# A pooling trunk layer: an opening that normalizes its operands before the first product

## The chip, the core and the metric

The kernel runs on one core of a Trainium2 chip. The core has a matrix engine (TensorE, PE in the profile; PEld is its weight load), a vector engine (VectorE, DVE), a scalar engine (ScalarE, ACT), GpSimd (POOL) and a queue engine (SyncE, SP) that here only issues transfers; ACT and POOL issue transfers too. On-chip data lie in SBUF, matmul results in eight PSUM banks of 128 x 512 float32. The metric is the time of one execution in microseconds; lower is better.

## What is computed

One layer: RMS norm, a causal pooling mixer with a gate, the residual, and a last RMS norm. The input `x` is 4096 x 1024 float32; the second mixer of the source is not used at this depth.

```python
def rms_norm(x, w):
    y = x * rsqrt(mean(x * x, axis=-1) + 1e-6)
    return y * w

def pool_mixer(h, in_w, group_w, group_b, scale, out_w):
    u, gate = split(h @ in_w, 2, axis=-1)                    # in_w: 1024 x 2048
    pooled = trailing_mean(u by group, windows 2/4/8/16) - u # 4 groups of 256 channels
    mixed = einsum('bsgc,gcd->bsgd', pooled, group_w) + group_b
    y = mixed * scale * silu(gate)
    return y @ out_w                                         # 1024 x 1024

h = x + pool_mixer(rms_norm(x, norm_w), ...)
out = rms_norm(h, final_norm_w)
```

## The kernel before

**Products.** Every float32 operand is split into a rounded part and a residual (`split`: an ACT copy of 128 x 1024, then a DVE subtraction), and a product is made of three matmuls (`mm3`). The large products follow Winograd's form of Strassen's scheme: seven block products, P1 to P7, in the order P1, P2, P6, P7, P5, P4, P3 (`ORDER_IN`). Steps "a" make the gate columns' half of the input product for four blocks of 1024 tokens, steps "b" the other half, and steps "o" the output product in eight blocks of 512 tokens. `group_w` is folded into `in_w` ahead (`fold`: matmuls of 128 x 256, line 334), because pooling acts on tokens and the group map on channels.

**One step.** `load`, `form` (the Strassen sums on DVE), `split_step`, `run` (`product_in`: eight groups of six matmuls, each group one half `h` of the inner dimension and one PSUM bank `ct`; then `evict_in`). P1 goes bank by bank, and its results are copied to banks 4 to 7 by the eviction, which frees banks 0 to 3 for P2 to add to. Bank 7 also serves as scratch for the spread below.

**Normalization.** The operands come transposed, with tokens along the free dimension, so each needs the factor of its token as a row that is equal in all partitions. `load_row` and `square_row` read `x` a second time, by rows, and sum its squares on ACT; `stats` and `rsqrt` make the factor (a root on ACT, the rest on DVE). In the first block `spread_rs` turns the factors of one half (512 tokens) into a row: an ACT copy and a DVE difference split them, two DVE products put them on a diagonal (`ident`), two matmuls with a matrix of ones (line 396) spread them into bank 7, and ACT copies them to `rstd`. Later blocks store and reload the factors through DRAM (`store_rs`, `load_rstd`), a block ahead.

**The opening before the change.** While weights arrive, 14 matmuls on zeros warm up PE. Eight folds of 16 matmuls follow: four with `gw[0]` and four with `gw[1]`, on weights `ru[q, k]` of 512 KB each, which take four buffers in turn. The operands of P1 and P2 of the first block (the first half's tokens) are used raw, without their factor; `evict_in` multiplies the results by the factor on DVE instead, and `normalize_raw` normalizes the operands afterwards for the Strassen sums and stores them to `sd` for steps "b". All loads go out on SP in the order of the program: the first half's rows (`load_row(0, 0, j)`) behind the third and fourth folds, then the second half's rows, P2's operand (`load(1)`), its weights (`g1`), and the four operands of P6 (`load(2)`). The first spread is written ahead of P1's second group, the second one ahead of its sixth.

**Order.** The program is written in one stream; a scheduler puts the instructions of each engine into an order, by the place in the program and by when it expects them to be ready. `tc.high_priority()` moves a part ahead; `tc.issue_after(i)` keeps a part behind instruction `i` on the same engine. Engines work through their queues in that order.

**The end.** The last block's rows are finished in halves: `late_factor` makes a row's factor, `late_half` applies it (one half on ACT, one on DVE) and stores both.

Of the kernel before, what the change touches and what calls it, by code (L numbers as in the profile page):

```python
# [10 lines left out]
F32 = mybir.dt.float32  # L11
# [49 lines left out]
def kernel(  # L61
# [82 lines left out]
    def sub(dst, a, b):  # L144
        nc.vector.tensor_tensor(out=dst, in0=a, in1=b, op=ALU.subtract)  # L145
# [7 lines left out]
    def split(dst, src):  # L153

        copy(dst[:, 0], src)
        sub(dst[:, 1], src, dst[:, 0].bitcast(F32))
# [30 lines left out]
    def rsqrt(dst, tmp, ms):  # L187

        nc.scalar.activation(tmp, ms, AF.Sqrt)
        nc.vector.reciprocal(out=dst, in_=tmp)  # L190
        mul(tmp, dst, ms)
        mul(tmp, tmp, dst)
        nc.vector.tensor_scalar(
            out=tmp, in0=tmp, scalar1=-0.5, scalar2=1.5, op0=ALU.mult, op1=ALU.add
        )
        mul(dst, dst, tmp)
# [111 lines left out]


# [10 lines left out]
    def load_wut(q, k, by=2):  # L320
        r = take("p (k t c) -> p k t c", early5, k=2, t=4)
        for kk in range(0, 2, by):
            nc.sync.dma_start(
                out=r[:, kk : kk + by],
                in_=wut[q, k + kk : k + kk + by].rearrange("k p t c -> p k t c"),
            )
        return r

    def fold(q, k, g, r, ps2, o, on_vector=False):

        for kk in range(2):
            for j in range(2):
                for t in range(2):
                    nc.tensor.matmul(  # L334
# [5 lines left out]
                    )  # L340
            if on_vector:
                last = nc.vector.tensor_scalar(
                    out=o[:, kk], in0=ps2[kk], scalar1=norm_c[k + kk], scalar2=None, op0=ALU.mult
                )
            else:
                last = nc.scalar.activation(o[:, kk], ps2[kk], AF.Copy, scale=norm_c[k + kk])
        give(r)
        return last
# [21 lines left out]
    def stats(b, half):  # L370
        ms = small.tile([P, 4], F32, tag="ms", name=f"ms{b}_{half}")
        nc.vector.tensor_scalar(
            out=ms, in0=sums[b, half], scalar1=1.0 / D, scalar2=EPS, op0=ALU.mult, op1=ALU.add
        )
        tmp = small.tile([P, 4], F32, tag="tmp", name=f"tmp{b}_{half}")
        rs = small.tile([P, 4], F32, tag="rs", name=f"rs{b}_{half}")
        rsqrt(rs, tmp, ms)
# [4 lines left out]

    def spread_rs(half, rs):

        hl = small.tile([P, 2, 4], F32R, tag="hl", name=f"hl{half}")
        split(hl, rs)
# [8 lines left out]
        for s in range(2):  # L395
            nc.tensor.matmul(
                banks[7], ones, r[:, s, 0], start=s == 0, stop=s == 1, skip_group_check=True
            )
# [24 lines left out]
    def split_halves(us, saved=None, by_pool=False):  # L423
        ts = []
        for h, u in enumerate(us):
            t = next_op("p (s a b) -> p s a b", s=2, a=2)
            split(t, u)
            if saved is not None:
                (nc.gpsimd if by_pool else nc.scalar).dma_start(out=saved[h], in_=u)
# [30 lines left out]
    def form_in(q, b, i):  # L460

        s = xs[b]
        if i in (P1, P2):
            if q == 0 and b > 0:
                for u in s["11" if i == P1 else "12"]:
                    normalize(b, 0, u)
        elif i == P6:
            s["2"] = [take(pool=early if q == 0 and b == 0 else None) for _ in range(2)]
# [16 lines left out]
    def split_in(q, b, i):  # L485
        s = xs[b]
        key = {P1: "11", P2: "12", P6: "2", P7: "21", P5: "11", P4: "22", P3: "12"}[i]
        raw = b == 0 and i in (P1, P2)
        t = split_halves(s[key], None if q or raw else sd[b].get(i), b == 0)
# [6 lines left out]

    def normalize_raw(i):

        for h, u in enumerate(xs[0]["11" if i == P1 else "12"]):
            normalize(0, 0, u)  # L500
            nc.gpsimd.dma_start(out=sd[0][i][h], in_=u)
# [7 lines left out]
    def mm3(ps, lt, r, start, stop):  # L509

        for n, (a, b) in enumerate(((lt[0], r[0]), (lt[0], r[1]), (lt[1], r[0]))):
            nc.tensor.matmul(  # L512
                ps, a, b, start=start and n == 0, stop=stop and n == 2, skip_group_check=True
            )
# [3 lines left out]
    def product_in(i, t, sets, by_bank, between=None):  # L518
# [4 lines left out]
        for n, (h, ct) in enumerate(halves):  # L523
# [3 lines left out]
            for kk in range(2):  # L527
                mm3(
                    ps[ct],
                    (w[i][h][:, 0, kk, c], w[i][h][:, 1, kk, c]),  # L530
                    (t[h][:, 0, kk], t[h][:, 1, kk]),
                    i in (P1, P7) and h == 0 and kk == 0,
                    h == 1 and kk == 1,
                )
# [81 lines left out]
    def evict_in(b, q, i, sets):  # L616
        ps = sets[bank_of[i]]
        last = None
        if i in (P1, P2) and b == 0 and q == 0:
            if i == P2:  # L620
                ev["11"] = [take() for _ in range(2)]
            for c, u in enumerate(sets["y"] if i == P1 else cells(ev["11"])):
                mul(u, ps[c], rstd[0][:, 0])
            if i == P2:
                for u in ev["11"]:
                    last = copy(u, u, AF.Silu)
# [526 lines left out]
```

## Time and profile before

| | |
|---|---|
| median of 3 runs | 966.03 us (965.89 to 967.31) |
| the profiled execution | 964.39 us; its span, first to last instruction, 962.6 us |
| PE busy | 949.7 us, 4190 matmuls |
| DVE, ACT busy | 748.4 and 453.0 us |
| POOL | 6.7 us, 16 instructions: 4 memsets and 12 transfers issued |
| transfers | 177.0 MB; in the first 62 us 23.8 MB |
| granted PE clock | 0.997 of full speed, mean |

The profile is of one execution. "Busy" is the time in which an engine had an instruction under way; matmuls are pipelined, so PE counts as busy while they follow each other. A line of a timeline is start, duration, engine, line of the kernel, operation, what it writes and reads, and how often; in brackets stands how long the engine was idle before and what ended that. Lines of helpers (142, 145, 148, 151) are shared by many uses, which the tile names tell apart: `op` is a split operand, `w` a weight, `st`, `vt` and `early` are buffers.

### The profile page before, as it was taken

Reading aid. Unit: us, or ns where it says so; the run is one execution under the profiler, and the core shown is the slowest. Engines: PE = TensorE matmul, PEld = TensorE weight load, DVE = VectorE, ACT = ScalarE, POOL = GpSimd, SP = SyncE. Lnnn points to the kernel's source line nnn. Section 1 sums busy time; section 2 is a strip of 40 time slices with the busy share of each in tenths; the row PEclk is TensorE's granted clock in tenths of the full one; section 3 lists DMA queues with packets and bytes.
Section 4 is the critical chain, followed back from the end, with each engine's and each line's share of the span. In section 5 each row is a group of like instructions: output and inputs, shape, how many; then the busy total and the mean of one; then the engine's idle time right before and its main releaser. Section 6 shows DMA issues by size and latency. Waiting matters only on the chain.

```text
span 962.6 us, 11058 instructions
## 1 busy us (share of the span) xinstructions
PE 949.7 (99%) x4190; PEld 785.5 (82%) x4190; DVE 748.4 (78%) x919; ACT 453.0 (47%) x677; POOL 6.7 (1%) x16
## 2 busy tenths in 40 slices
PE   9999999999999999999999999999999999999996
PEld 8778888888888888888888888888888888888885
DVE  4699994893895997696697599499978667677675
ACT  5849447347445555345345445553423424324233
POOL 0110000000000000000000000000000000000000
PEclk9999999999999999999999999999999999999998
DMA  9965864564656646016614733645746436356022
GB/s 337 408 264 157 305 237 163 210 240 137 213 219 226 233 156 237 1 45 218 240 44 165 263 119 131 219 151 178 259 141 212 162 123 230 108 187 218 22 88 88
DMA packets 67685, 177.01 MB, mean 184 GB/s; under 512 B 6704, under 2 KB 24240, under 8 KB 67632
## 3 DMA queue, kind: packets, MB, share of 16 engines
q1 hardware_dynamic: 61728, 156.37, 46.8%
q10 hardware_dynamic: 4176, 13.65, 3.5%
q0 software_dynamic: 1728, 6.29, 1.6%
q8 instruction: 33, 0.54, 0.2%
q14 instruction: 20, 0.16, 0.1%
HBM read 116.50 MB, written 59.78 MB: 183 GB/s over the span
## 4 chain that ended last, share of the span: by engine, by line
PE 78%; DVE 13%; DMA 5%; ACT 3%; issue 1%; DVEq 0%; SPq 0%; ACTq 0%
PE bank L512 75%; PE bank L334 2%; DVE op L145 2%; DVE vt L142 2%; DMA st<-wvd 2%; DVE st L148 1%; DVE st L145 1%; DMA rd<-rs 1%; DVE st L598 1%; DVE w L145 1%; DMA st<-rd 1%; DVE st L261 1%; DVE vt L145 1%; DVE w L209 1%; DVE st L142 1%
## 5 line engine op out<-in xcount | busy, mean ns | idle before, releaser
L512 PE MATMUL bank<-op,w 128*128 128x512 f32 x2688 | 611.7, 389 | 2.5 <-ACT op L151 2.1
L512 PEld LDWEIGHTS bank<-op,w 128*128 128x128 f32 x2688 | 504.0, 188 | 109.1 <-ACT op L151 2.6
L512 PE MATMUL bank<-w,op 128*128 128x512 f32 (+1 forms) x1356 | 305.0, 387 | 0.0
L512 PEld LDWEIGHTS bank<-w,op 128*128 128x128 f32 x1356 | 253.0, 188 | 52.0
L151 ACT ACTIVATE op<-st 128x1024 fp32r<-128x1024 f32 x117 | 123.2, 1056 | 142.0 <-PE bank L512 112.2
L145 DVE TENSOR_TENSOR op<-st,op 128x1024 fp32r<-128x1024 f32 x117 | 141.5, 1217 | 38.7 <-ACT op L151 38.3
L151 ACT ACTIVATE op<-vt 128x1024 fp32r<-128x1024 f32 x49 | 51.8, 1059 | 92.2 <-PE bank L512 72.9
L142 DVE TENSOR_TENSOR vt<-vt 128x1024 f32<-128x1024 f32 (+6 forms) x72 | 87.7, 1227 | 0.1
L142 DVE TENSOR_TENSOR st<-bank,st 128x512 f32<-128x512 f32 x78 | 53.1, 686 | 36.9 <-PE bank L512 36.6
L145 DVE TENSOR_TENSOR op<-vt,op 128x1024 fp32r<-128x1024 f32 x49 | 59.8, 1220 | 21.7 <-ACT op L151 21.7
L151 ACT ACTIVATE vt<-bank 128x512 f32<-128x512 f32 x90 | 52.6, 595 | 46.1 <-PE bank L512 42.5
L142 DVE TENSOR_TENSOR vt<-bank,vt 128x512 f32<-128x512 f32 (+1 forms) x83 | 55.1, 677 | 15.0 <-PE bank L512 10.8
L145 DVE TENSOR_TENSOR st<-st,st 128x1024 f32<-128x1024 f32 x35 | 42.3, 1217 | 13.0 <-DMA st<-wvd 11.2
L151 ACT ACTIVATE bank<-bank 128x512 f32<-128x512 f32 x44 | 25.5, 582 | 33.9 <-PE bank L512 30.1
L145 DVE TENSOR_TENSOR w<-st,w 128x1024 fp32r<-128x1024 f32 x22 | 26.5, 1220 | 16.4 <-ACT w L151 16.2
L148 DVE TENSOR_TENSOR st<-st,st 128x1024 f32<-128x1024 f32 (+1 forms) x18 | 20.4, 1160 | 19.6 <-DMA st<-rd 18.3
L151 ACT ACTIVATE w<-st 128x1024 fp32r<-128x1024 f32 x22 | 23.1, 1059 | 22.9 <-PE bank L512 15.4
L151 ACT ACTIVATE st<-bank 128x512 f32<-128x512 f32 x36 | 21.2, 596 | 21.1 <-PE bank L512 19.1
L593 DVE SCALAR_TENSOR_TENSOR vt<-vt,vt 128x1024 f32<-128x1024 f32 x24 | 29.2, 1217 | 0.1
L334 PE MATMUL bank<-early,early 128*128 128x256 f32 x128 | 27.8, 379 | 0.0
L334 PEld LDWEIGHTS bank<-early,early 128*128 128x128 f32 x128 | 24.3, 190 | 3.3
L598 DVE SCALAR_TENSOR_TENSOR st<-vt,colt,st 128x512 f32<-128x512 f32 x36 | 25.6, 742 | 0.0
(116 smaller groups left out, 449.7 us busy)
## 6 DMA issues: line engine op xcount, KB each, us to landing
st<-in_x SPq DMA_DIRECT2D x34, 512.0 KB, 4.5
vt<-in_x SPq DMA_DIRECT2D x25, 512.0 KB, 4.5
st<-sd SPq DMA_DIRECT2D x25, 512.0 KB, 5.4
st<-in_xt SPq DMA_DIRECT2D x24, 512.0 KB, 6.1
sd<-st ACTq DMA_DIRECT2D x19, 512.0 KB, 6.4
st<-yd SPq DMA_DIRECT2D x19, 512.0 KB, 3.7
yd<-st SPq DMA_DIRECT2D x18, 512.0 KB, 2.9
out<-st SPq DMA_DIRECT2D x17, 512.0 KB, 4.8
```

What stands on the lines that cost most here:

```text
L142: nc.vector.tensor_tensor(out=dst, in0=a, in1=b, op=ALU.add)
L145: nc.vector.tensor_tensor(out=dst, in0=a, in1=b, op=ALU.subtract)
L148: nc.vector.tensor_tensor(out=dst, in0=a, in1=b, op=ALU.mult)
L151: return nc.scalar.activation(dst, src, func)
L209: nc.vector.scalar_tensor_tensor(out=dst[:, 1], in0=u, scalar=c, in1=dst[:, 0].bitcast(F32), op0=ALU.mult, op1=ALU.subtract,)
L261: nc.vector.scalar_tensor_tensor(out=u[:, j], in0=u[:, j], scalar=cs[j], in1=other[:, j], op0=ALU.mult, op1=op)
L334: nc.tensor.matmul(ps2[kk][:, j * 256 : (j + 1) * 256], r[:, kk, 2 * j + t, :], g[:, 2 * j + t, :], start=(t == 0), stop=(t == 1),)
L512: nc.tensor.matmul(ps, a, b, start=start and n == 0, stop=stop and n == 2, skip_group_check=True)
L593: nc.vector.scalar_tensor_tensor(out=s[:, :, at : at + H], in0=s[:, :, at : at + H], scalar=1.0 / win, in1=v[:, :, HIST:], op0=ALU.mult, o ...
L598: nc.vector.scalar_tensor_tensor(out=sg[:, j], in0=s[:, j, at : at + H], scalar=bias_c[2 * grp + j], in1=sg[:, j], op0=ALU.add, op1=ALU.mult,)
```

## The change

- **Operands of P1 and P2** are normalized before they are split, as in the other blocks; the DVE products in `evict_in` and `normalize_raw` are gone. `split_halves` stores the normalized operands to `sd` at once, on POOL's queue.
- **Loads.** The first half's four rows go out ahead of the last weights of the first four folds, the identity and `gw[1]`; `in_w`'s rows later. The first fold weights are issued half on ACT's queue and half on SP, ahead of `cols`. P2's operand and weights now go out ahead of the second half's rows.
- **Factors.** The first half's squares stand behind the first fold, the first spread behind the sixth fold's matmuls. The second spread is written behind P1 and held behind its last matmul; P2's second group is held behind it (`behind`).
- **Root.** A root on one column at the start brings its table in; `rsqrt` takes mean and epsilon into the root itself and does its multiplications on POOL, one reciprocal on DVE. `rsqrt` serves all blocks and the output's norm.
- **Folds.** Outputs are taken after the weights' buffer is given back; in the last four folds DVE evicts one of the two banks. 8 warm-up matmuls instead of 14.
- **Later weights.** P7's residuals, and the weights made in the first block's steps, are held on DVE behind the latest operand split.
- **End.** The second row half of P4 is finished behind the factor of P3's first row half, and DVE's part of `late_half` is held behind the latest addition or mean.

```diff
-    for c in range(14):
+    for c in range(8):
...
+    scrap = const.tile([P, 1], F32, name="scrap")
+    nc.scalar.activation(scrap, eps, AF.Sqrt)
+    def rsqrt(dst, tmp, ms, ss):
+        nc.scalar.activation(tmp, ss, AF.Sqrt, bias=eps, scale=1.0 / D)
+        nc.gpsimd.tensor_scalar(
+            out=ms, in0=ss, scalar1=1.0 / D, scalar2=EPS, op0=ALU.mult, op1=ALU.add
+        )
         nc.vector.reciprocal(out=dst, in_=tmp)
-        mul(tmp, dst, ms)
-        mul(tmp, tmp, dst)
-        nc.vector.tensor_scalar(
+        nc.gpsimd.tensor_tensor(out=tmp, in0=dst, in1=ms, op=ALU.mult)
+        nc.gpsimd.tensor_tensor(out=tmp, in0=tmp, in1=dst, op=ALU.mult)
+        nc.gpsimd.tensor_scalar(
             out=tmp, in0=tmp, scalar1=-0.5, scalar2=1.5, op0=ALU.mult, op1=ALU.add
         )
-        mul(dst, dst, tmp)
+        nc.gpsimd.tensor_tensor(out=dst, in0=dst, in1=tmp, op=ALU.mult)
...
     def spread_rs(half, rs):
-        split(hl, rs)
+        copy(hl[:, 0], rs)
+        nc.gpsimd.tensor_tensor(
+            out=hl[:, 1], in0=rs, in1=hl[:, 0].bitcast(F32), op=ALU.subtract
+        )
...
+        with tc.issue_after(latest[0]):
+            for s in range(2):
+                spread_done[0] = nc.tensor.matmul(
+                    banks[7], ones, r[:, s, 0], start=s == 0, stop=s == 1, skip_group_check=True
+                ).ins
...
-        raw = b == 0 and i in (P1, P2)
-        t = split_halves(s[key], None if q or raw else sd[b].get(i), b == 0)
+        t = split_halves(s[key], None if q else sd[b].get(i), b == 0)
...
+            with tc.issue_after(behind) if behind and n == 1 else nullcontext():
...
-        if i in (P1, P2) and b == 0 and q == 0:
-            if i == P2:
-                ev["11"] = [take() for _ in range(2)]
-            for c, u in enumerate(sets["y"] if i == P1 else cells(ev["11"])):
-                mul(u, ps[c], rstd[0][:, 0])
-            if i == P2:
-                for u in ev["11"]:
-                    last = copy(u, u, AF.Silu)
-        elif i == P1:
+        if i == P1:
...
+                if i == P3 and j == 0:
+                    late_half(*partial.pop("waiting"))
+        if final and i == P4:
+            partial["waiting"] = (half, 1, n, factors.pop())
...
-    ru[0, 0] = load_wut(0, 0, by=1)
-    for h, k in chunks[1:]:
-        ru[0, k] = load_wut(0, k)
-    g0.append(load_rows(in_w, 0, D))
-    gw[1] = load_group_w(1)
+    ru[0, 0] = load_wut(0, 0, (nc.scalar, nc.sync))
+    nc.scalar.dma_start(out=colt, in_=cols)
+    ru[0, 4] = load_wut(0, 4)
+    ru[0, 2] = load_wut(0, 2)
+    load_row(0, 0, 0)
+    load_row(0, 0, 1)
+    ru[0, 6] = load_wut(0, 6)
+    load_row(0, 0, 2)
+    load_row(0, 0, 3)
     ident = take(pool=early)
     nc.sync.dma_start(out=ident.rearrange("p a b -> p (a b)")[:, 0:P], in_=eye)
+    gw[1] = load_group_w(1)
     for n, (h, k) in enumerate(chunks):          # the first four folds
...
         ru[1, k] = load_wut(1, k)
         if n == 0:
             load(0)
+            for j in range(4):
+                square_row(0, 0, j)
+            with tc.high_priority():
+                rs = stats(0, 0)
+        elif n == 1:
+            for hh in range(2):
+                g0.append(load_rows(in_w, 2 * hh, D))
...
-    for j in range(4):
-        load_row(0, 1, j, early if j < 1 else None)
     load(1)
     g1 = [load_rows(in_w, 4 + 2 * h, D) for h in range(2)]
+    for j in range(4):
+        load_row(0, 1, j, early if j < 3 else None)
+    load(2)
...
     for n, (h, k) in enumerate(chunks):          # the last four folds
+        o = fold(1, k, gw[1], ru[1, k], banks[2 * (n % 2) : 2 * (n % 2) + 2], early5, (0,))
         nc.gpsimd.dma_start(out=wvd[k // 2], in_=o)
         give(o)
+        if n == 0:
+            for hh in range(2):
+                split_scaled(w[P1][hh], g0[hh], pair(norm_c, hh, 0))
+        elif n == 1:
+            with tc.high_priority():
+                spread_rs(0, rs)
+            form(0)
+            split_step(0)
+            second_side(0)
     give(gw[1])
+    second_side(1)
+    form(1)
     split_step(1)
     for h in range(2):
         split_scaled(w[P2][h], g1[h], pair(norm_c, h, 1))
+    for j in range(4):
+        square_row(0, 1, j)
+    with tc.high_priority():
+        rs = stats(0, 1)
+    def spread_second():
+        with tc.high_priority():
+            spread_rs(1, rs)
-    run(0, {1: lambda: spread(0), 5: lambda: spread(1)})
+    run(0, {8: spread_second})
...
     for h in range(2):
         for key in ("21", "22"):
-            normalize(0, 1, xs[0][key][h])
-    form(2)
-    split_step(2)
-    run(1)
-    normalize_raw(P2)
+            normalize(0, 1, s[key][h])
+        sub(s["21"][h], s["11"][h], s["21"][h])
+        sub(s["2"][h], s["22"][h], s["21"][h])
+        split_up[2] += split_halves([s["2"][h]])
     give(rstd.pop(0))
+    run(1, behind=spread_done[0])
     for h in range(2):
-        split(w[P7][h], v0[h])
-        give(v0[h])
+        copy(w[P7][h][:, 0], v0[h])
+    with tc.issue_after(latest_split[0]):
+        for h in range(2):
+            sub(w[P7][h][:, 1], v0[h], w[P7][h][:, 0].bitcast(F32))
+            give(v0[h])
...
         if kind == "a" and b == 0:
-            rest_of_first(n)
+            with tc.issue_after(latest_split[0]):
+                rest_of_first(n)
```

## The prediction

> **What bounds the kernel now.** I read the page first, then what TensorE waited for, then the opening in order of time.
>
> ```profile
> PE 949.7 (99%) x4190; PEld 785.5 (82%) x4190; DVE 748.4 (78%) x919; ACT 453.0 (47%) x677; POOL 6.7 (1%) x16
> ```
>
> PE is busy for 949.7 of 962.6 us and no product is removed, so the change can win only from the 12.9 us in which PE is idle. The waits of PE (engine, line, releaser: us in total, times, longest) place 5.2 us of them; 7.7 us lie behind the last matmul (954.9 to 962.6).
>
> ```profile
> PE bank L512 <- ACT op L151: 2.1, 1, 2.1
> PE bank L900 <- DVE op L898: 1.5, 1, 1.5
> PE bank L396 <- DVE w L389: 1.2, 1, 1.2
> PE bank L512 <- DVE op L145: 0.4, 2, 0.2
> ```
>
> The timeline of PE from 30 to 62 us (start, duration, instruction, idle before):
>
> ```profile
> 33.84 1.72 PE L512 MATMUL bank<-op,w 128*128 128x512 f32 x6
> 36.80 0.50 PE L396 MATMUL bank<-w,w 128*128 128x512 f32 x1 [1.24 <-DVE w L389]
> ...
> 37.74 10.86 PE L512 MATMUL bank<-op,w 128*128 128x512 f32 x47
> ...
> 49.25 9.49 PE L512 MATMUL bank<-op,w 128*128 128x512 f32 x41
> 60.88 1.42 PE L512 MATMUL bank<-op,w 128*128 128x512 f32 x5 [2.14 <-ACT op L151]
> ```
>
> PE stands 1.24 us for the first spread (L396) and 2.14 us before P6, which ends at 72.6. From there to 955 it waits 0.4 us at most, so what is won at P6's end is won for the program. Why P6 waited is in the windows (busy PE, PEld, DVE, ACT, POOL; clock; DMA share; GB/s) and the timeline of DVE:
>
> ```profile
> 50.00:54.00 4.00, 4.00 (x19) 3.32 (x18) 4.00 (x6) 1.36 (x2) 0.00 (x0) 1.00 1.04 410
> 58.00:62.00 4.00, 1.86 (x9) 1.14 (x7) 4.00 (x5) 3.46 (x5) 0.59 (x2) 1.00 0.99 405
> ```
> ```profile
> 51.37 1.22 DVE L148 TENSOR_TENSOR vt<-vt,st 128x1024 f32<-128x1024 f32 x1
> 52.50 3.49 DVE L148 TENSOR_TENSOR st<-st,st 128x1024 f32<-128x1024 f32 x3
> ```
>
> The second spread is done at 50.4; then DVE does four normalizations and four differences at 1.22 us one after the other, and P6's operand is the last. DMA is full as well (about 410 GB/s from 30 to 60 us), so 512 KB (0.524 MB) more ahead of a load make it land 1.28 us later. The DMA view, asked in windows around single issues, gives issue to landing (13.1 us for the last two rows of the second half, issued at 22.8 and 23.8; 16.1 for the last loads of P6's operand, issued up to 37.5):
>
> ```profile
> vt<-in_x SPq DMA_DIRECT2D x2, 512.0 KB, 13.1
> st<-in_xt SPq DMA_DIRECT2D x3, 512.0 KB, 16.1
> ```
>
> So the second half's rows have landed by 37.4 (13.65 for the last one alone) and the last operand by 53.6.
>
> **The change part by part.**
>
> *Start.* Warm-up loses 6 matmuls at 0.23 us, 1.4 us; one half of the first weights goes out on ACT's queue at 0.7 instead of SP's at 1.8, ahead of `cols`, which is needed only at the first eviction (8.3). The folds can begin near 5.3 instead of 6.4. But four row loads now stand ahead of fold weights: the seventh block landed 5.5 us after its issue at 16.96, at 22.5, and lands 4 x 1.28 = 5.1 us later, at 27.6, less about 0.5 for the earlier start, 27.1. In the trace that fold begins at 6.41 + 6 x 3.46 = 27.2 (16 matmuls at 0.216 each). It begins no earlier now, and the folds end near 27.1 + 6.9 = 34.0, where they ended at 34.2. The 1.1 us is lost again; nothing to 1.1 is the range.
>
> *First factors.* The first rows land by 15 (nine blocks of 512 KB at 1.28 us, from 3), four squares at 1.24 us are hidden under folds, the spread follows fold 6 at about 27. Then one ACT copy of 0.6, two normalizations of 1.22, two splits (ACT 1.05, DVE 1.22): ready near 33, beside folds. DVE has 9.8 us of work between 24.3 (first `in_w` rows) and 34. P1 starts on the folds and its stop of 1.24 us is gone, as are the 0.36 and 0.3 us in which PE turned between spread and product. With 48 matmuls at 0.227 us, 10.9 us, P1 ends near 44.9 (now 47.2, after 6, 1 and 41 of the 47 matmuls above). Cover gone, each us by which DVE is late costs one. The eight evictions of 0.69 us on DVE become ACT's (0.6 each) and shorten no wait by themselves. The table load (1.28 us, at 33.2) goes from ACT's chain to the start, where another stood.
>
> *Second factors.* This is what is late next. Their rows move behind four loads (two operands, two weight tiles), 4 x 1.28 = 5.1 us, and the stores of P1's and P2's inputs, until now put off, share the engines earlier; with the wvd stores up to four more have gone by then, again 5.1. The rows land between 42.5 (no store ahead) and 47.6 (all ahead); I take 47.0, as POOL's queue has the stores ready from 24 to 38. Then square 1.24, root 0.2, reciprocal 0.17, four small POOL operations, factor copy 0.21, two products of 0.65 and hand-overs of 0.1: with 0.2 us for a POOL operation 4.6 us, so the spread is at 51.6 and the factors are there at 52.7. PE does not idle all of 44.9 to 51.6: four of P2's eight groups (6 matmuls, 1.36 us each) depend on neither the spread nor bank 7's eviction, and today's order shows that late work is passed: the second spread is written ahead of P1's sixth group and runs behind P2's first. So P2 runs to 50.3, waits 1.3, spreads 0.5, and ends near 57.5 (now 58.7).
>
> *P6.* From 52.7: two normalizations, two differences (4 x 1.22) and the ACT copy of 1.05 give its first operand at 58.6, its residual 1.2 later; the second half follows 5 DVE steps later, at 64.7 plus 1.2, where PE's first 5.4 us are done at about 65.2. P6 ends near 71.4, against 72.6: 1.2 us won. DVE's slots are free for this: P2's evictions leave it.
>
> *POOL.* Five small operations of each of two factor chains here, six later ones and 14 output chains go from DVE (0.16 to 0.19 us each) to POOL, whose page shows no such operation. Its nearest rows are 0.10 us for a 128x1 memset and 0.53 for issuing a store. I take 0.2, as both are short and the data is 4 columns; the range runs from 0.1 to 1.2 for a start and a hand-over that these rows do not show, and for store issues ahead in its queue. In the later blocks nothing waits: the factors go through DRAM there (4.5 and 5.1 us) and PE never stood.
> By the Trainium skill's GPSIMD Engine Reference, section 4.1, elementwise work belongs on the Vector engine, since POOL is about twice as slow for two inputs. That gives an estimate of 0.33 us, and the second factors would come about 0.5 us later; no operation of this trace can confirm it.
>
> *Waits by order.* `behind` holds P2's second group until the spread: priced above. `latest_split` puts weight splits behind operand splits on DVE, where P7 is 11 us away: nothing. If that cover went, a split is 1.22.
>
> *End.* DVE's last chain stands behind a 0.75 us product: the square root ends at 956.8, the reciprocal starts at 957.25.
>
> ```profile
> 956.46 0.75 DVE L798 SCALAR_TENSOR_TENSOR st<-st,columns,st 128x512 f32<-128x512 f32 x1
> 956.50 0.29 ACT L780 ACTIVATE columns<-columns 128x1 f32<-128x1 f32 x1
> ...
> 957.25 0.15 DVE L782 RECIPROCAL columns<-columns 128x1 f32<-128x1 f32 x1
> ```
>
> The P4 half moves behind the next factor chain, which frees 0.7 us earlier: I take 0.3 (nothing to 0.45).
>
> **Sum.** 1.2 + 0.3 = 1.5 us. The profiled execution took 964.4 us (span 962.6, 1.8 around it) and becomes 962.9; it lies 1.6 us below the median of 966.0, which becomes 964.5.
>
> **Rivals.**
> 1. *All hidden.* Stores give way, the rows land at 42.5, the spread fits P1's end. P2 ends at 56.2, P6 waits only for its last loads (53.6 plus one store, 54.9) and ends near 68.7: 3.9 us, with the end 4.2, 961.8. For: `behind` fits such a time. Against: a full DMA.
> 2. *PE queued behind the spread.* If it is placed after P2's first group, PE waits from 46.3 to 51.6 and does seven groups after it: P2 ends at 61.6, P6 at 72.7; with the end 965.8 (966.6 for rows at 47.6).
> 3. *POOL is slow* (slower). Five steps of the second chain are on POOL. At p us each P6 ends 5(p - 0.2) later: the gain of 1.5 is gone at p = 0.5, and 0.2% slower is reached at 0.9. At 1.2 us it costs 5, so 969.5. For: no row shows such an operation, and POOL also issues eight stores in that stretch. Against: its memset of 0.1 us.
> 4. *Folds on a slow PE.* The first eight warm-up matmuls are 0.43 us apart, the rest 0.23; eight may just not be enough. Sixteen folds at half speed cost 3.5 us, of which the lead of 1.1 pays part, and all later stages move by up to 2.4: 965 to 967.
> The Trainium skill's TensorE: Matmul & The Clock Gate, Part 1, says that the warm-up takes about 3.4 us of time in a window that runs freely; eight at 0.43 are just that, and by this rule it may go either way.
>
> **Numbers.** Chances: forecast 0.37, all hidden 0.23, queued 0.14, slow POOL 0.20, slow folds 0.06. A measurement of this kernel can tell about 0.2%, 1.9 us, from no change. Faster by more is "all hidden" and a third of the forecast (below 964.1): 0.35. Slower by more is slow POOL and the upper ends of cases 2 and 4: 0.23. The rest, 0.42, is within. The likeliest case alone spans 963.5 to 966 (rows at 45 to 47.6). The range leaves out the lower half of case 1 and the upper half of case 3: 961.9 to 968.5.
>
> **What the profile would show.** Right: folds that wait for weights in their second half and end at 34; no PE wait at P1's start; squares of the second half's rows at 45 to 48; a PE wait of 1 to 3 us in P2 released by DVE's factor products; P6 starting near 58.6; POOL operations near 0.2 us. Wrong: rows landing at 43 or a P2 without a wait (case 1), one matmul group between P1 and the spread (case 2), POOL operations over 0.5 us (case 3), 0.43 us between folds (case 4), or a PE wait after 75 us that is not there today, which no term here covers.

## The result: slower

The changed kernel takes 970.63 us (median of 6 runs, 969.34 to 972.84), the kernel before on the same chip 966.28 (965.19 to 967.31): a ratio of 1.0049, 95% interval 1.0035 to 1.0063. The forecast was 964.5, the range ended at 968.5. The profiled execution took 969.63 us, its span 967.9, against 962.6 before. PE now stands 16.2 us instead of 12.9, and some of its work runs at half clock.

The page's busy times and what PE waited for (engine, line, releaser: us in total, times, longest), of the changed kernel:

```profile
PE 951.7 (98%) x4184; PEld 785.5 (81%) x4184; DVE 733.5 (76%) x804; ACT 451.9 (47%) x679; POOL 46.2 (5%) x128
```
```profile
PE bank L525 <- DVE op L145: 2.6, 3, 2.1
PE bank L525 <- DVE early L359: 1.6, 1, 1.6
PE bank L525 <- ACT early L363: 1.5, 1, 1.5
PE bank L910 <- DVE op L908: 1.5, 1, 1.5
PE bank L348 <- DVE early L359: 1.5, 1, 1.5
```

The two old stops (1.24 us for the first spread, 2.14 before P6) are gone, as forecast. Three new ones stand in the opening; all three are released by the eviction of a fold (L359, L363). The timeline of PE there, and what held those evictions (waits of DVE and of ACT, DVE's timeline, and the DMA view around the fifth fold's store):

```profile
26.86 0.81 PE L415 MATMUL bank<-w,w 128*128 128x512 f32 x2
27.58 3.69 PE L348 MATMUL bank<-early,early 128*128 128x256 f32 x16
32.76 3.72 PE L348 MATMUL bank<-early,early 128*128 128x256 f32 x16 [1.49 <-DVE early L359]
38.02 0.96 PE L525 MATMUL bank<-op,w 128*128 128x512 f32 x3 [1.54 <-ACT early L363]
40.61 14.00 PE L525 MATMUL bank<-op,w 128*128 128x512 f32 x54 [1.63 <-DVE early L359]
54.45 0.39 PE L415 MATMUL bank<-w,w 128*128 128x512 f32 x1
```
```profile
DVE early L359 <- DMA wvd<-early: 5.0, 1, 5.0
ACT early L363 <- DMA wvd<-early: 3.6, 1, 3.6
```
```profile
31.95 0.75 DVE L359 TENSOR_SCALAR early<-bank,colt 128x512 f32<-128x512 f32 x1 [5.03 <-DMA wvd<-early]
...
33.94 2.35 DVE L148 TENSOR_TENSOR st<-st,st 128x1024 f32<-128x1024 f32 x2
```
```profile
wvd<-early POOLq DMA_DIRECT2D x1, 512.0 KB, 7.5
```

Read from the bottom: the fifth fold's output was handed to its store at 24.33 us, and the store landed 7.5 us later. Its buffer had been given back at once, and the sixth fold's output took it. So that eviction waits until 31.9, on both engines, and DVE works in order: the normalization of P1's operand, whose factors have lain ready since 28.3, stands behind it until 33.94. The first product starts at 38.02 instead of 33.84.

Then the clock. Windows of the changed kernel (busy PE, granted clock, DMA share, GB/s):

```profile
36.88:40.29 3.41, 0.96 (x3) 1.00 1.03 419
40.29:43.71 3.42, 3.10 (x7) 0.50 1.03 420
```

In the first of these PE worked 0.96 of 3.41 us, in short bursts between the waits; for the next 3.41 us it is granted half its clock, worth 1.7 us of matmuls. No single stop was longer than 1.63 us.

How late the large products are against the kernel before, comparing the starts of the same matmul in the two profiles (us; blocks are counted from 1, and the second column is the start in the changed kernel less that in the kernel before):

| matmul, and its time before | later by |
|---|---|
| first of P1, 33.8 | +4.2 |
| end of P1, 47.1 | +5.4 |
| first of P6, 60.9 | +3.1 |
| within P6, 66.8 | +2.7 |
| block 3, 198.0 | +3.8 |
| steps b, first block, P6, 367.2 | +5.7 |
| last matmul, 954.6 | +5.7 |
| end of the span | +5.2 |

So 2.7 us come from the opening, 3.0 from places that the sum didn't touch, 1.9 of them just ahead of the matmul at 367.2 (372.9 in the changed kernel), and the end gives 0.5 back. The timeline of PE there, changed kernel, where PE waited 0.19 us before the change:

```profile
372.90 282.95 PE L525 MATMUL bank<-op,w 128*128 128x512 f32 x1247 [2.09 <-DVE op L145]
```

### The profile page after: what moved, and what is told of

Its sections match the earlier page's. It is cut to its first block, busy times and chain, and to the rows that moved or that the text cites. A ratio compares the mean times of both kernels' runs of the same rounds, so it can differ in the third digit from the quotient of the medians.

```text
span 967.9 us, 11092 instructions
## 1 busy us (share of the span) xinstructions
PE 951.7 (98%) x4184; PEld 785.5 (81%) x4184; DVE 733.5 (76%) x804; ACT 451.9 (47%) x679; POOL 46.2 (5%) x128
## 4 chain that ended last, share of the span: by engine, by line
PE 77%; DVE 13%; DMA 5%; issue 2%; ACT 2%; POOL 0%; ACTq 0%; DVEq 0%; POOLq 0%; SPq 0%
PE bank L525 74%; DVE op L145 3%; DVE vt L142 2%; PE bank L348 2%; DMA st<-wvd 2%; DVE st L148 1%; DVE st L145 1%; DMA rd<-rs 1%; DVE w L145 1%; DVE st L614 1%; DMA wvd<-early 1%; DMA st<-rd 1%; DVE w L219 1%; DVE st L271 1%; DVE vt L609 1%
## 5 line engine op out<-in xcount | busy, mean ns | idle before, releaser
L151 ACT ACTIVATE op<-st 128x1024 fp32r<-128x1024 f32 x119 | 125.5, 1056 | 147.1 <-PE bank L525 135.9
L145 DVE TENSOR_TENSOR op<-st,op 128x1024 fp32r<-128x1024 f32 x119 | 144.4, 1220 | 50.3 <-ACT op L151 49.9
L151 ACT ACTIVATE op<-vt 128x1024 fp32r<-128x1024 f32 x47 | 49.7, 1058 | 87.4 <-PE bank L525 83.3
L151 ACT ACTIVATE vt<-bank 128x512 f32<-128x512 f32 x94 | 54.8, 596 | 49.4 <-PE bank L525 44.7
L145 DVE TENSOR_TENSOR op<-vt,op 128x1024 fp32r<-128x1024 f32 x47 | 57.4, 1221 | 20.7 <-ACT op L151 20.7
L823 DVE TENSOR_TENSOR st<-bank,st 128x512 f32<-128x512 f32 x60 | 41.2, 689 | 41.1 <-PE bank L525 40.9
L151 ACT ACTIVATE bank<-bank 128x512 f32<-128x512 f32 x48 | 27.5, 579 | 28.9 <-PE bank L525 24.6
L197 POOL TENSOR_SCALAR oms<-oss 128x2 f32<-128x2 f32 x14 | 9.7, 691 | 641.2 <-ACT st L734 636.7
L823 DVE TENSOR_TENSOR vt<-bank,vt 128x512 f32<-128x512 f32 (+1 forms) x37 | 24.9, 674 | 16.3 <-PE bank L525 16.3
L142 DVE TENSOR_TENSOR vt<-bank,vt 128x512 f32<-128x512 f32 x48 | 31.7, 683 | 0.1
```

What stands on the lines that cost most here:

```text
L142: nc.vector.tensor_tensor(out=dst, in0=a, in1=b, op=ALU.add)
L145: return nc.vector.tensor_tensor(out=dst, in0=a, in1=b, op=ALU.subtract)
L151: return nc.scalar.activation(dst, src, func)
L197: nc.gpsimd.tensor_scalar(out=ms, in0=ss, scalar1=1.0 / D, scalar2=EPS, op0=ALU.mult, op1=ALU.add)
L823: partial["added"] = nc.vector.tensor_tensor(out=u[:, c], in0=ps[j][:, c], in1=u[:, c], op=ALU.add).ins
```

## Experiments

All ratios are against runs of the kernel before on the same chip; the chip differs between some experiments, and a ratio is not exactly the quotient of two medians (they differ by up to 0.12%), so differences of 0.1% are not read. "Lag" is the start of a matmul in a kernel's profiled execution less that of the same matmul in the profile of the kernel before. "Kernel 3" is the kernel of experiment 3.

**1. Own buffers for the folds' outputs.** A buffer whose store is in flight is not given back until all folds are done:

```diff
+    stored = []
     for n, (h, k) in enumerate(chunks):
         o = fold(1, k, ...)
         nc.gpsimd.dma_start(out=wvd[k // 2], in_=o)
-        give(o)
+        stored.append(o)
...
+    for o in stored:
+        give(o)
```

> The changed kernel with one edit: the output buffers of the last four folds are given back after the fourth fold, not after each, so that each fold's output takes the buffer of its own weights and not the one whose store to DRAM is under way. Theory 'buffer' (the evictions of the sixth fold wait for the store of the fifth fold's output, 3.6 us on ACT and 5.0 us on DVE, and everything queued behind them on DVE waits too): these two waits and PE's 1.5, 1.5 and 1.6 us are gone, the first product starts near 34.5 us (38.0 now), P6 starts near 60 us (64.0 now), and the time is 964 to 967 us, 3 to 6 below the changed kernel's 970.6. Rival 'late rows' (what was forecast: the second half's rows and the factors made of them bound the opening): the first product starts early too, but PE then waits in P2 for the spread and P6 still starts at 62 us or later: 968.5 us or more. Rival 'POOL' (the small operations on POOL cost the time): no change, 970 to 971 us.

Measured: 972.14 us, 1.0059 (1.0045 to 1.0073). The mechanism held, the time didn't: no eviction waits for `wvd`, P1 starts at its old time (lag -0.2) and is 1.5 us ahead in its middle. But then PE waits 3.15 us between P1 and P2, its clock is halved, and it leads no more. Later it stalls for 2.5 us at 372.7, and the clock is halved once more. Removing the first cause uncovers a second one in the same stretch.

**2. The same buffers in the kernel before.** Its opening is left as it is; only the last four folds' outputs are taken from the weights' buffers after these are given back, as in the change, and evicted on ACT.

> The kernel before with one part of the change alone: in the last four folds the output buffer is taken after the weights' buffer is given back, out of the same four buffers (both banks evicted on ACT behind the whole fold). Theory 'buffer': the eviction of the sixth fold waits on ACT for the store of the fifth (issue to landing 7 to 8 us), 4 to 6 us of ACT's queue, which is full there; the first spread comes that much later and PE waits: 969 to 973 us. Rivals 'late rows' and 'POOL': this part does nothing by itself, 965.5 to 967 us.

Measured: 979.45 us, 1.0129 (1.0111 to 1.0146): the direction was right, the size too small. PE waits 5.0, 2.7, 2.5 and 2.4 us at four places, and the clock is halved for 13.6 us in all. This edit alone breaks the kernel before, too.

**3. Own buffers, and the factors' arithmetic back on DVE.** As 1, and the four multiplications, the mean and the difference `hl` on `nc.vector` instead of `nc.gpsimd`.

> As after_own_buffers, and the small multiplications of rsqrt and of the first factors' split are back on DVE instead of POOL. Theory 'buffer': POOL was no part of the loss; within 1 us of after_own_buffers. Rival 'POOL': 2 us or more faster than after_own_buffers.

Measured: 968.59 us, 1.0019 (1.0008 to 1.0031), 0.4% better than 1, more than the "within 1 us" of theory 'buffer'. The gain isn't in the opening (P6's lag is +2.7, worse than 1's +1.2): the stalls near 197 and 372 us are gone. What is left in the opening is one wait, and this is what stands ahead of its end on ACT (timelines of PE and ACT):

```profile
50.35 4.39 PE L525 MATMUL bank<-op,w 128*128 128x512 f32 x11 [4.35 <-ACT bank L151]
```
```profile
48.66 1.06 ACT L381 ACTIVATE vt<-vt 128x1024 f32<-128x1024 f32 x1 [1.40 <-DMA vt<-in_x]
49.63 0.19 ACT L381 ACTIVATION_READ_ACCUMULATOR vt<-vt 128x1 f32 x1
49.72 0.58 ACT L151 ACTIVATE bank<-bank 128x512 f32<-128x512 f32 x1
```

P2 adds to banks that P1's evictions (`bank<-bank`) must clear; on ACT these stand behind the squares of the second half's rows, and the last row landed at 48.64. PE's 11 matmuls afterwards take 4.39 us: half clock.

**4. The rows first.** As 1, with the second half's rows issued ahead of P2's operand and weights.

> As after_own_buffers, and the four rows of the second half are loaded ahead of P2's operand and weights again, as in the kernel before. 'Late rows': their squares come about 5 us earlier, the second spread too, and P6 starts 2 to 4 us earlier than in after_own_buffers: 961 to 964 us. Without it: P2's operand and weights come 5 us later and P2 waits for them instead, no gain or 1 to 3 us slower than after_own_buffers.

Measured: 969.23 us, 1.0025 (1.0011 to 1.0038). It is 0.3% better than 1, which fits neither theory: P6 starts 2 us later than in 1 (lag +3.3), and the gain comes from 372 us, where PE waits only 0.32 us. In the opening the squares are done by 38.9, but P2's weights land at 45.8 to 49, and the factor's copy on ACT now stands behind their splits: PE waits 3.84 us for the spread. There the order of the loads only chose who was late.

**5. Only the later roots on POOL, in the kernel before.** Blocks 2 to 4 and the output's norm as in the change; opening and end as before.

> The kernel before, its opening and its end untouched: only the factor chains of blocks 2 to 4 and of the output rows are made as in the changed kernel (root straight from the sum of squares, four multiplications and the mean on POOL, one reciprocal on DVE). Theory 'POOL's chains cost time later': the stalls of 1 to 2.5 us at the first product of block 2 (near 197 us) and at the first product of steps b (near 372 us), with a half clock behind them, appear here too; 2 to 4 us above the kernel before. Rival 'only with the new opening': the later stages are unchanged, within 0.6 us of the kernel before.

Measured: 971.12 us, 1.0036 (1.0024 to 1.0047), as the theory expected. The lag grows from +2.3 at 350 us to +5.8 at 367 us, where PE waits 2.48 us for a split operand; 1.6 of it stand since the opening, which the edit doesn't touch. None of these waits is released by an operation on POOL.

**6. The changed kernel with all roots on DVE.**

> The changed kernel with its buffers as they are; only the multiplications of all factor chains and the difference of the factors' two parts are back on DVE. Theory 'the two costs add up': the opening stays about 3 us late (sixth fold's eviction waits for a transfer, half clock behind it), the later 2 to 3.5 us go: 0.1 to 0.25% above the kernel before, 967.2 to 968.7 where that takes 966.3. Rival 'POOL matters only with the outputs' own buffers': no better than the changed kernel, 0.45% above the kernel before.

Measured: 969.24 us, 1.0023 (1.0011 to 1.0035), so about half of the 0.49% goes with the roots: the costs add up. The wait at 371 us is 0.29.

**7. P1's evictions ahead of the squares.** As 3, with three of P1's evictions issued before the squares (`issue_after`), and P2's fourth group held behind the spread instead of its second:

```diff
-    run(0, {8: spread_second})
+    product_in(P1, split_up.pop(0), p1, True)
+    for c in range(3):
+        copied = copy(p1["y"][c], p1["x"][c])
+    with tc.issue_after(copied.ins):
+        for j in range(4):
+            square_row(0, 1, j)
```

> The changed kernel with own buffers for the last folds' outputs and all roots on DVE (0.19% above the kernel before), and besides: the first three evictions of P1 stand ahead of the second half's squares on ACT, and P2's fourth group instead of its second is held behind the second spread. Theory 'ACT's queue': the wait of 4.35 us between P1 and P2 and the half clock behind it go, as three groups of P2 (4.1 us) run while the rows are still on their way; P6 starts 2.5 to 4 us earlier, 964 to 966 where the kernel before takes 966.3. Rival 'late rows': the spread is no earlier, PE only waits at another place, 3 to 4 us ahead of the spread, and the clock halves there: within 1 us of the kernel that it is made from, 967 to 969.

Measured: 967.37 us, 0.9999 (0.9985 to 1.0013). The wait of 4.35 us is gone and P6 starts 1.9 us ahead, and yet the kernel is level: within P6 the lead is lost to DVE's eight steps (P6's second operand), and at 120 us the lag is +1.4. There DVE had stood 5.1 us idle, as it does in the changed kernel. Timelines of DVE, the kernel before and the changed one:

```profile
97.83 1.23 DVE L148 TENSOR_TENSOR st<-st,vt 128x1024 f32<-128x1024 f32 x1 [1.15 <-DMA vt<-rd]
```
```profile
94.72 1.23 DVE L148 TENSOR_TENSOR st<-st,vt 128x1024 f32<-128x1024 f32 x1 [4.80 <-DMA vt<-rd]
```

It is the first normalization of block 2, which waits for factors that are still on their way through DRAM. Before, it stood behind the splits of P4's operand, two weight splits and P5's four additions; now it stands ahead of them.

**8 and 9. That normalization behind P3's operand split**, in kernel 7 and alone in the changed kernel.

> The changed kernel with own buffers, roots on DVE and P1's evictions first (level with the kernel before: 0.9999), and besides: the first normalization of block 2 stands behind the operand split of P3 on DVE instead of ahead of it. Theory 'DVE stands behind a factor that is still in DRAM': its idle 5.1 us at 87 to 92 us fall to under 1.5, the waits of PE between 94 and 118 us (0.8) go, and the lead of P6's start (1.9 us, of which 1.8 were lost within P6) is no longer turned into a lag of 1.4 us at 120 us: 0.8 to 2.5 us faster than the kernel that it is made from, so 964.6 to 966.4 where the kernel before takes 967.1. Rival 'DVE is full up to 372 us anyway': PE's waits only move to 190 or 372 us; within 0.5 us of the kernel that it is made from.

> The changed kernel with one edit: the first normalization of block 2 stands behind the operand split of P3 on DVE instead of ahead of it. Theory 'DVE stands behind a factor that is still in DRAM': DVE's idle 4.8 us before 94.7 us shrink to under 1.5, the lag behind the kernel before stays near 2.7 us from 70 to 200 us instead of growing to 3.8, and the stall of 2.1 us at 372 us gets shorter: 0.1 to 0.3% faster than the changed kernel, 0.2 to 0.4% above the kernel before. Rival 'covered': the lag grows as it did, within 0.05% of the changed kernel's 0.45 to 0.5%.

Measured: with 7, 965.06 us, 0.9977 (0.9964 to 0.999), faster than the kernel before; alone, 970.9 us, 1.0035 (1.0022 to 1.0048), not to be told from the changed kernel's 1.0049. The wait for the factors is gone in both (DVE waits 3.2 us for ACT there instead), and the lag at 120 us falls from 3.5 to 2.9 in the second; a stall of 2.5 us at 372 us eats that. It mattered only where nothing later was worse.

**10 and 11. The stores put off.** Back to kernel 3, without 7 and 8. The first attempt wrote the four `sd` stores behind P2 in the program, on POOL's queue:

> The changed kernel with own buffers for the last folds' outputs and all roots on DVE (0.19% above the kernel before), and besides: the four stores of P1's and P2's operands are issued behind P2's product, as late as in the kernel before. Theory 'full transfers': four times 1.28 us less ahead of the second half's rows, which land 2.5 to 5 us earlier; the wait of 4.35 us between P1 and P2 falls to 0 to 2 us and trips no half clock: 963.5 to 966 where the kernel before takes 966.3. Rival 'the rows' order, not the stores': rows less than 1 us earlier, within 1 us of the kernel that it is made from.

It tested nothing: nothing stood ahead of them there, and they went out at 29.9, 31.0, 40.8 and 42.0 us as before (969.89 us, 1.0017, 1.0001 to 1.0033). The second one holds them:

```diff
     run(1, behind=spread_done[0])
+    with tc.issue_after(evicted[0]):
+        for i, key in ((P1, "11"), (P2, "12")):
+            for h in range(2):
+                nc.scalar.dma_start(out=sd[0][i][h], in_=xs[0][key][h])
```

> The changed kernel with own buffers for the last folds' outputs and all roots on DVE (0.19% above the kernel before), with the four stores of P1's and P2's operands now held on ACT's queue behind P2's evictions; in the run after_stores_later they still went out at 29.9, 31.0, 40.8 and 42.0 us, so that run didn't test them. Theory 'full transfers': two stores (of 1.28 us each) that were ahead of the rows' landing are gone, the last rows land at 46 to 47 instead of 48.6 us, and the wait of 4.35 us between P1 and P2 falls to 2 to 3 us: 0.1 to 0.25% faster than the kernel that it is made from, 965.5 to 967.5 where the kernel before takes 967. Rival 'ACT's queue': the eviction copies still stand behind the last square, the wait stays over 3.5 us and within 0.08% of the kernel that it is made from.

Measured: 963.18 us (962.23 to 964.6), 0.9971 (0.9959 to 0.9982), the best of all, and more than its theory expected. Issue to landing of the last row, in kernel 3 and here (DMA views around its issue), then PE and ACT here:

```profile
vt<-in_x SPq DMA_DIRECT2D x1, 512.0 KB, 20.3
```
```profile
vt<-in_x SPq DMA_DIRECT2D x1, 512.0 KB, 15.2
```
```profile
34.81 10.95 PE L526 MATMUL bank<-op,w 128*128 128x512 f32 x47 [0.54 <-DVE early L359]
45.96 2.79 PE L526 MATMUL bank<-op,w 128*128 128x512 f32 x11 [0.20 <-ACT bank L151]
48.59 0.40 PE L415 MATMUL bank<-w,w 128*128 128x512 f32 x1
```
```profile
45.24 0.19 ACT L381 ACTIVATION_READ_ACCUMULATOR vt<-vt 128x1 f32 x1
45.33 0.58 ACT L151 ACTIVATE bank<-bank 128x512 f32<-128x512 f32 x1
```

The row lands at 43.31 instead of 48.64, so ACT's queue runs through and the 4.35 us are 0.20. The 5.3 us are those of all four stores (4 x 1.28 = 5.1), not of the two that the theory counted. The spread is done 6 us earlier (48.6), P6 starts 3.25 us ahead of the kernel before and doesn't wait, and the clock never halves before the last matmul. The order on ACT that 7 changed did no harm once the rows were in time.

**12. Both cures.** Kernel 8 with the stores held:

> The fastest kernel so far (own buffers, roots on DVE, P1's evictions first, block 2's first normalization later: 0.9977 of the kernel before), with the four stores of P1's and P2's operands held on ACT's queue behind P2's evictions. Theory 'full transfers': the rows land some 2 us earlier, the spread no longer makes PE wait (0.9 us) and P6 starts about 1 to 2 us earlier: ratio 0.996 to 0.997. Rival 'given back later': the stores then share the engines with the rows and operands of block 2 and with P6's late loads, or P6's second operand is bound by DVE's eight steps anyway: ratio 0.9975 to 0.9985.

Measured: 965.31 us, 0.9993 (0.998 to 1.0006). The held stores and P1's evictions first don't add up: P6 starts 2.5 us ahead, but 1.8 of it are lost within P6 (waits of 0.64 and 0.90 us), and more at 116 us (0.79) and 368 us (1.23).

**13 and 14. What each is worth without the others.** The stores held in the changed kernel and nothing else; then own buffers and the stores held, with POOL's roots as in the change.

> The changed kernel with one edit: the four stores of P1's and P2's operands are held on ACT's queue behind P2's evictions; last folds' buffers and POOL's roots as in the change. Theory 'the latest of two': P1 still starts at 38 us, as a fold waits for its buffer's transfer, and ends at 51 to 52.4, and the earlier rows only take away what stood behind it: P6 starts 0.5 to 2 us earlier, 0.05 to 0.2% faster than the changed kernel, 0.25 to 0.45% above the kernel before. Rival 'stores alone': as much as with own buffers and DVE roots, 0.45% faster than the changed kernel, level with the kernel before.

> The changed kernel with own buffers for the last folds' outputs and the four stores held behind P2's evictions; only POOL's roots are left of what was taken for the three causes (all three mended gave 0.9971 of the kernel before). Theory 'three causes that add up': POOL's chains cost 2 to 3.5 us, in the stalls near 197 and 372 us; ratio 0.999 to 1.001. Rival 'POOL's stalls come from a late opening only': with P6 early there is slack at 372 us, no stall over 0.5 us there, ratio 0.9965 to 0.998.

Measured: the stores alone, 971.96 us, 1.0046 (1.0032 to 1.0061), nothing against 1.0049. In its profile, of the slowest of its ten runs, the rows land at 42.1, but the sixth fold's eviction still waits, for 6.4 us on DVE, and P1 starts at 39.3. Own buffers and stores, 965.63 us, 0.9983 (0.9971 to 0.9994): with POOL's roots left, P6 is 1.5 us ahead, not 3.25, and the stall near 368 us is there (2.35 us; lag from -1.3 at 198 us to +0.9 behind it). The stall speaks against the rival, which expected none over 0.5 us there. The time doesn't decide: 0.9983 lies between the two ranges expected, and its interval overlaps kernel 11's.

The ladder, ratio to the kernel before:

| folds' buffers | stores | roots on POOL | roots on DVE |
|---|---|---|---|
| as changed | as changed | 1.0049 | 1.0023 |
| as changed | held | 1.0046 | not run |
| own | as changed | 1.0059 | 1.0019 |
| own | held | 0.9983 | 0.9971 |

Buffers or stores alone are worth nothing, both together 0.5 to 0.7%. Roots on POOL cost 0.3% in the first row and 0.4% in the third; the 0.1% of the last row is not clear of the noise.

## Why the prediction was wrong, step by step

**Start.** Right in what it looked at. The folds began at 5.07 (forecast 5.3), the first at half clock until 6.16. The seventh block of weights landed at 27.5 (27.1), and PE waited 0.2 us for weights. The first spread ran at 26.86 (near 27). The "sixteen folds at half speed" of rival 4 can only be the sixteen matmuls of one fold (3.46 us): there are eight folds.

**The step that failed first: "the folds end near 34.0".** The sum knew one release for a fold, its weights, and took the output's buffer as free. That "outputs are taken after the weights' buffer is given back" stood in the description of the change and was costed nowhere. The pool of free buffers is a queue that hands out the one given back first: the sixth fold got the fifth's output, whose store was in flight, and not the buffer that its own weights had just left. With the transfers full, that store took 7.5 us. The folds ended at 36.5, the operand was ready at 39.2 instead of 33, and P1 ended at 52.4, not 44.9: 7.5 us of error, of which the late start is 4.0, one more stop 1.6 and the half clock 1.7. No rival had it.

**Second factors.** The bounds were good: rows at 42.5 without stores ahead and 47.6 with all of them; measured 45.7 in the changed kernel, where the late evictions put the stores off by accident, 48.6 with all ahead (experiment 3), and 42.1 to 43.7 with none (11 to 14). The spread came at 54.45 (51.6). What was missed is the price of late rows: the 6.7 us between P1's end and the spread were thought to be covered by P2's free groups, but P1's evictions are needed by all of them and queue on ACT behind the squares. That "four of P2's eight groups" depend on neither the spread nor bank 7's eviction was no cover in this order (experiments 1 and 3; in the changed kernel itself P1 ended too late for it to show).

**Rival 1 (all hidden)** had the right mechanism and nearly the right price, for another kernel: with the stores out of the way P6 gains 3.25 us (it said 3.9 at its end), and 963.18 us were measured where it said 961.8. The change brings this time only if its stores are put off and its buffers are free.

**P6.** It starts at 63.98 (58.6), without the wait before it, so 3.1 us later than before.

**POOL.** Three of the five operations of an output chain take 0.19 to 0.20 us on average, as taken; the other means are 0.3 to 0.7. In the second factor chain it took 2.4 us from the root to the first product, 1.7 with DVE. Rival 3 looked in the wrong place: the opening shows no steady price (with the roots on POOL P6 starts 1.3 us later in the changed kernel than in 6, 1.5 us earlier in 1 than in 3). A stall of 2.1 to 2.5 us near 372 us, though, stands in six of the seven kernels with POOL's roots and in two of the nine others. Groups of the changed kernel (count, then busy us and mean ns, then idle time before them):

```profile
L201 POOL TENSOR_TENSOR tmp<-rs,ms 128x4 f32<-128x4 f32 x8 | 4.5, 560 | 19.7 <-DVE rs L200 19.7
L206 POOL TENSOR_TENSOR ors<-ors,otmp 128x2 f32<-128x2 f32 x14 | 2.8, 197 | 1.2
```

The Trainium skill's GPSIMD Engine Reference, section 4.1, puts elementwise work on the Vector engine; the estimate of 0.33 us that the prediction drew from it was above most of these operations. In the three pairs of the ladder the roots on DVE were faster, or not to be told apart.

**"In the later blocks nothing waits."** This was the second false step: a lack of PE waits after 75 us was read as slack. Before the change PE waited only 0.19 us at 367 us, so its operand came just in time, and DVE was busy for 35.0 of the 36 us from 340 to 376. So the 2 us by which DVE was later in the changed kernel appear whole. The prediction named "a PE wait after 75 us that is not there today, which no term here covers" as what would make it wrong, and it came.

The traces show where DVE gets late. It is at the first normalization of block 4, which waits for factors from DRAM (DVE, kernel before and changed kernel):

```profile
258.74 1.23 DVE L148 TENSOR_TENSOR st<-st,st 128x1024 f32<-128x1024 f32 x1 [2.65 <-DMA st<-rd]
```
```profile
261.06 1.23 DVE L148 TENSOR_TENSOR st<-st,st 128x1024 f32<-128x1024 f32 x1 [5.29 <-DMA st<-rd]
```

In all seven kernels with POOL's roots it stands four operations further ahead in DVE's order than in the nine others, and DVE idles 4.7 to 5.5 us there with that work behind it, against 1.9 to 3.7. In the changed kernel the last store of `yd` ahead of the folded weights then leaves SP at 291.59 instead of 284.65, those weights (`wvd`) go out 5.3 us later where PE lags by 3.8, and the last one that DVE waits for lands at 320.41 instead of 314.52; from there DVE is nearly full up to the stall. So the price is that of an order, as at block 2 in 8 and 9, and not of slow operations on POOL. This is read from the traces; no run puts that normalization back with the roots on POOL. Nor is it the only way to the stall: kernels 2 and 10, with the roots on DVE, have one of 2.4 and 2.5 us (in 10 the last of these loads took 6.7 us instead of 5.7). Kernel 4, with POOL's roots and weights as late, has only 0.32 us; DVE's order behind them is another one there.

**"What is won at P6's end is won for the program"** fails both ways: a lag of 2.7 us became 5.7, and a lead of 3.2 us (11) became 1.6.

**End.** Forecast 0.3; from the last matmul's start to the end 7.49 us instead of 7.97, so 0.48. The product (L802) now runs ahead of the last root, so the reciprocal follows the root's end at 962.51 by 0.08 us, where it stood 0.46 us behind it before (DVE and ACT, changed kernel; L781 is the root, L785 the reciprocal):

```profile
961.81 0.74 DVE L802 SCALAR_TENSOR_TENSOR st<-st,columns,st 128x512 f32<-128x512 f32 x1
962.22 0.29 ACT L781 ACTIVATE columns<-columns 128x1 f32<-128x1 f32 x1
962.47 0.21 DVE L758 TENSOR_SCALAR columns<-columns 128x1 f32<-128x1 f32 x1
962.59 0.15 DVE L785 RECIPROCAL columns<-columns 128x1 f32<-128x1 f32 x1
```

## What to carry to other kernels

When an edit moves where a buffer is taken or given back, ask for each taker what is still reading that buffer, and cost the wait with the landing time of a transfer at that moment, not with its size: here 7.5 us for 512 KB. On full transfers a store that nobody waits for is not free, it is paid by the next load that somebody waits for; hold it until that load has landed, and make sure that the edit really holds it. An engine without waits isn't an engine with slack: here a wait of 0.19 us at 367 us said that the operand came just in time. And when operations leave an engine, look at the order of what is left on it: an operation that waits for DRAM can move ahead of work that is ready.

## What the runs showed of the hardware

The half clock doesn't need a long stop. In all 16 profiles the granted clock changes on a grid of 3.41 us. Ahead of the last matmul, every such stretch at full clock with PE busy for 1.32 us or less (13 of them) was followed by one at half clock, and none with 1.51 us or more was. So waits of 1.5 and 1.6 us around a short burst cost a further 1.7 us in the changed kernel, and a wait of 2.5 us cost that or nothing (373 us in experiments 1 and 5), as the grid happened to lie.

The Trainium skill's TensorE: Matmul & The Clock Gate, Part 1, names a free-running window of 3.4 us, and the trace agrees; it asks for a whole idle window before the clock falls, where these runs show 0.96 us of work in 3.41 (the windows above) that didn't prevent it. The measurement decides.
